# A 1-core transformer block: the first two modulation parts summed on TensorE in four column tiles, x loaded first, the first weights in narrower pieces

## The chip, the cores and the metric

The kernel runs on one core of a Trainium2 chip. The metric is device time in microseconds (us) of one execution, as the median of several. A profile of one execution gives the times of single instructions. Engines: TensorE (PE; its weight loads are PEld), VectorE (DVE), ScalarE (ACT), GpSimd (POOL) and SyncE (SP), which issues nearly all DMA transfers. Every engine works off its own list of instructions in order, so an instruction that waits holds up all that stand behind it on that engine.

## The reference, cut to what matters

Two layers of a block with D = 1024 and 256 tokens, all in float32. Each layer starts with six modulation rows made from a condition vector `c`; the first two (shift and scale) are needed before the first product of the mixer.

```python
cond = jax.nn.silu(c)                                  # [1, 1024]
mod = cond @ w_mod[l] + b_mod[l]                       # [1, 6*1024]; w_mod[l] is 1024 x 6144
sh1, sc1, g1, sh2, sc2, g2 = jnp.split(mod, 6, axis=-1)
h = _modulate(_rmsnorm(x, norm1_w[l]), sh1, sc1)       # norm * (1 + sc1) + sh1
y = _mixer(h, w_in[l], ...)                            # projections of h, three recurrent/attention branches
x = x + g1[:, None, :] * y
...                                                    # then a dense FFN (layer 0) or an 8-expert MoE (layer 1)
```

## The kernel before

Weights stream from HBM through a pool of four buffers `rawa` of 8 KB a partition (1 MB each), in the order in which units of work consume them. `Stream.loads` (L90) issues a load on SP as soon as a buffer is released; the order in which the instructions of different kinds follow one another on an engine is set by a scheduler when the program is built. The modulation weights of later parts go through two smaller buffers `rawm` (0.5 MB each).

A product with float32 weights is split in two: ACT copies a piece of weights to a rounded `wh` (L112), DVE subtracts to get the rest `wl` (L113), and TensorE sums three products (L517 to L519 with the activations first, L530 to L532 with them second). There are four pairs of `wh`/`wl`, and a unit of 256 output columns takes two of them, so the pairs of the next unit are made while TensorE works on this one. A unit has 48 matmuls. The first units are two of `b_f` (evacuated to `bf`), two of `b_q` (`bq`), two of `b_i` (`bi`), two of `b_g` (`bg`).

The start of the program, before the first product:

- `setup_cond` loads `c`, transposes it and forms `csil` = silu(c) (L278, L279). `setup_loads` (L283 to L288) brings norm weights and biases through six small transfers on POOL's queue; `setup_cols` transposes them (L292, L293) and ACT copies them to `pcol` and `bcol` (L294, L295).
- Parts 0 and 1 of layer 0: eight slices of 128 rows of `w_mod` each, two slices to a transfer of 1 MB (the last two of part 1 come singly). DVE adds each slice, times its entry of `csil`, into `macc` (L391, L393), eight operations of 128x1024 a part. `mod_done` then transposes `macc` in eight pieces on TensorE (L429), sums over the partitions on DVE (L430) and adds the bias (L431); after part 1 it forms `acol` (L435).
- Between them stands the norm of x: four squares with sums on ACT (`nsq`, L452), one sum on DVE (`nst`, L457), one power on POOL (`rr`, L273), two scaled identities on ACT (`dg`, L461), and 16 float32 products on TensorE that transpose and scale x (L473; the trace has two rows for each).
- `norm_T` applies `acol` and `modc` (`hf`, L486 on DVE and L488 on ACT) and splits the result in `hh` (ACT, L499) and `hl` (DVE, L500). The first product is L517.

A little later the first recurrent branch starts (`hgrn`, L592 to L600): ACT forms `he` in three steps (absolute value, exp, ln), DVE forms `hls` and `hkf` from it, ACT takes exp of `hkf`, and TensorE multiplies it (L630). Each change of function table on ACT is an instruction of its own, ACT_TABLE_LOAD. `setup_late`, which runs between the units, has some small exp and ln of its own (`lsm`, `lbe`).

The rest of the program (the mixer of layer 0, its FFN, the mixer of layer 1 and the experts) is in the same order before and after the change.

Of the kernel before, what the change touches and what calls it, by code (L numbers as in the profile page):

```python
# [15 lines left out]
OP = mybir.AluOpType  # L16
# [174 lines left out]
def _body(ctx, tc, nc, I, out):  # L191
# [76 lines left out]
    def rsqrt(pool, ss, n, scale, name):  # L268
# [5 lines left out]
        return r  # L274

    def setup_cond():
        p = ps_x()
        PE.transpose(out=p[:, 0:8], in_=prow2[0:8, :], identity=ident[0:8, 0:8])  # L278
        A.activation(out=csil, in_=p[:, 0:8], func=AF.Silu)  # L279

    def setup_loads():
# [93 lines left out]
    def mod_subs(l, part, ring, per, early=False):  # L375
# [3 lines left out]

        def step(k):  # L380
            def fn(src):
                if k == 0:
                    if l == 0 and part < 2:
                        st["acc"] = pools["s"].tile([128, D], F32, name="macc", tag="s")
                    else:
                        st["acc"] = pools["mac"].tile([128, D], F32, name="macc", tag="macc")
                    if part in (2, 5):
                        G.memset(st["acc"], 0.0)
                        SP.dma_start(out=st["acc"][0:1, :], in_=I["b_mod"][l:l + 1, part * D:(part + 1) * D])
# [5 lines left out]
                if k == 7:  # L395
                    if l == 0 and part < 2:
                        done(st["acc"])
                    else:
                        late.append([MD, lambda: done(st["acc"])])
            return fn  # L400
# [77 lines left out]
    def norm_T(pool, ps, l, which, dst):  # L478

        for j, pv in enumerate(ps):  # L480
# [8 lines left out]
            dst(j, hf)  # L489

    cur = {}

# [544 lines left out]
    def layer_mixer(l):  # L1037
# [7 lines left out]

        def t_unit(key, name, evac):
            raw = wchunk(W, COL[key], 512)

# [23 lines left out]
        def act(func):  # L1072
            return lambda o, i: A.activation(out=o, in_=i, func=func)
# [10 lines left out]

        seq = []
        r, f = t_unit("bf", "b_f", act(AF.Copy))
        cols_units(r, f, pre=lambda: norm_h(pools, l, 0))
        r, f = t_unit("bq", "b_q", act(AF.Silu))
# [569 lines left out]

    stream.unit([], first_norm, mods=list(mod_subs(0, 0, "a", 2)), alone=True)
    stream.unit([], lambda hi, lo: None, mods=list(mod_subs(0, 1, "a", 2, True)), alone=True)  # L1660
    n_mix = 2
# [16 lines left out]
    with tc.manual_schedule():  # L1678
        setup_cond()
        stream.loads()  # L1680
        SP.dma_start(out=x, in_=I["x"].rearrange("o (b p) d -> p (o b) d", p=128))
        setup_loads()
        setup_cols()
        stream.run(2, tick)
# [56 lines left out]
```

## Time and profile before

| | us |
|---|---|
| three runs | 1644.56, 1646.06, 1650.3 (median 1646.06) |
| the profiled execution | 1643.47 |
| its span, first to last instruction | 1641.8 |
| TensorE busy in the span | 1535.2 (94%) |
| VectorE, ScalarE, GpSimd busy | 764.9, 575.7, 42.5 |
| first weight product (L517) starts | 36.37 |

The span and the busy times are of the one profiled execution, which is 2.6 us faster than the median of the three runs; 1.67 us of it lie outside the span.

### The profile page before, as it was taken

The page shows a single profiled execution, that of the slowest core. Times are in us where ns is not written, and L with a number is a line of the kernel's source. Part 1 is how long each engine was busy: PE and PEld are TensorE (multiplying, and loading weights), DVE is VectorE, ACT ScalarE, POOL GpSimd, SP SyncE. Part 2 cuts the span into 40 slices and gives each one's busy share as a digit, 9 for nine tenths or more (in the row PEclk, how much of TensorE's full clock was granted, in tenths as well). Part 3 has the DMA queues.
Part 4 walks back from the last instruction along what each step waited for, and adds up shares of the span by engine and source line. Part 5 has one row for each costly group of instructions (what it writes and reads, how often), then busy time and mean ns, then how long its engine had stood idle before and what let it go on. Part 6 is the DMA issues. An engine that isn't in the chain of part 4 may idle for free. (4 is left out here: it accounts for less than half of the span.)

```text
span 1641.8 us, 25655 instructions
## 1 busy us (share of the span) xinstructions
PE 1535.2 (94%) x10586; PEld 1069.2 (65%) x10586; DVE 764.9 (47%) x1226; ACT 575.7 (35%) x904; POOL 42.5 (3%) x54
## 2 busy tenths in 40 slices
PE   3999999989999899999997999999999988987997
PEld 2999899989998899999996333433334322322332
DVE  7898788755877559865764010211012111111201
ACT  3576557645444487765752010100001000100000
POOL 2001020000000000001000000000000000000000
PEclk9999999999999999999998999999999999999999
DMA  9656777436789633654467799999899999999990
GB/s 361 231 177 217 244 267 259 155 103 226 240 296 320 228 129 129 219 168 154 155 214 299 260 352 354 407 406 321 319 329 407 403 408 405 407 403 407 404 372 36
DMA packets 162776, 459.25 MB, mean 280 GB/s; under 512 B 11454, under 2 KB 19716, under 8 KB 162600
## 3 DMA queue, kind: packets, MB, share of 16 engines
q1 hardware_dynamic: 162408, 456.55, 75.7%
q8 instruction: 140, 2.29, 0.6%
q14 instruction: 36, 0.29, 0.1%
q0 software_dynamic: 192, 0.11, 0.0%
HBM read 455.58 MB, written 1.05 MB: 278 GB/s over the span
## 5 line engine op out<-in xcount | busy, mean ns | idle before, releaser
L1463 PE MATMUL pm<-rawa,xg 128*64 128x512 f32 (+2 forms) x2368 | 417.8, 522 | 21.1 <-DMA rawa<-in_moe_w 18.6
L113 DVE TENSOR_TENSOR wl<-rawa,wh 128x1024 fp32r<-128x1024 f32 (+1 forms) x243 | 293.9, 1215 | 103.1 <-ACT wh L112 102.2
L112 ACT ACTIVATE wh<-rawa 128x1024 fp32r<-128x1024 f32 (+1 forms) x243 | 255.2, 1054 | 229.9 <-PE pm L518 117.3
L1463 PEld LDWEIGHTS pm<-rawa,xg 128*64 128x64 f32 (+1 forms) x2368 | 141.6, 131 | 280.0 <-issue 225.9
L517 PE MATMUL pm<-hh,wh 128*128 128x256 f32 x992 | 285.4, 288 | 4.8 <-ACT hh L499 4.6
L518 PE MATMUL pm<-hl,wh 128*128 128x256 f32 x992 | 283.8, 287 | 0.9 <-DVE hl L500 0.9
L519 PE MATMUL pm<-hh,wl 128*128 128x256 f32 x992 | 283.0, 286 | 1.5 <-DVE wl L113 1.5
L517 PEld LDWEIGHTS pm<-hh,wh 128*128 128x128 f32 x992 | 189.0, 191 | 8.1 <-ACT hh L499 4.8
L519 PEld LDWEIGHTS pm<-hh,wl 128*128 128x128 f32 x992 | 189.1, 191 | 2.4 <-DVE wl L113 1.9
L518 PEld LDWEIGHTS pm<-hl,wh 128*128 128x128 f32 x992 | 189.3, 191 | 1.9 <-DVE hl L500 1.4
L1463 PE MATMUL px<-rawa,gt 128*64 128x512 f32 x704 | 168.0, 600 | 12.5 <-DMA rawa<-in_moe_w 12.3
L1534 DVE TENSOR_TENSOR esg<-esg,pm 128x512 f32<-128x512 f32 (+1 forms) x48 | 29.5, 641 | 297.7 <-PE pm L1463 297.4
L531 PE MATMUL pm<-wl,hh 128*128 128x256 f32 x448 | 128.7, 287 | 1.6 <-DVE wl L113 1.6
L530 PE MATMUL pm<-wh,hh 128*128 128x256 f32 x448 | 128.8, 288 | 0.0
L532 PE MATMUL pm<-wh,hl 128*128 128x256 f32 x448 | 127.8, 285 | 0.0
L1463 PEld LDWEIGHTS px<-rawa,gt 128*64 128x64 f32 x704 | 46.1, 136 | 107.8 <-issue 83.8
L393 DVE SCALAR_TENSOR_TENSOR macc<-rawm,csil,macc 128x1024 f32<-128x1024 f32 x74 | 94.6, 1279 | 30.8 <-DMA rawm<-in_w_mod 30.1
L531 PEld LDWEIGHTS pm<-wl,hh 128*128 128x128 f32 x448 | 85.1, 190 | 2.0 <-DVE wl L113 1.8
L1561 DVE COPY ys<-pm 128x512 f32<-128x512 f32 x8 | 5.5, 691 | 173.2 <-PE pm L1463 93.9
L532 PEld LDWEIGHTS pm<-wh,hl 128*128 128x128 f32 x448 | 85.0, 190 | 0.2 <-issue 0.2
L530 PEld LDWEIGHTS pm<-wh,hh 128*128 128x128 f32 x448 | 85.0, 190 | 0.0
L1497 ACT ACTIVATE gt<-px 128x512 f32<-128x512 f32 (+1 forms) x24 | 13.5, 564 | 197.3 <-PE px L1495 197.3
(370 smaller groups left out, 1940.6 us busy)
## 6 DMA issues: line engine op xcount, KB each, us to landing
rawa<-in_moe_w SPq DMA_DIRECT2D x216, 1024.0 KB, 17.1
rawa<-in_w_in SPq DMA_DIRECT2D x68, 1024.0 KB, 6.3
rawa<-in_moe_w SPq DMA_DIRECT2D x64, 768.0 KB, 12.0
rawm<-in_w_mod SPq DMA_DIRECT2D x80, 512.0 KB, 7.6
rawa<-in_ffn_w SPq DMA_DIRECT2D x29, 1024.0 KB, 7.6
rawa<-in_w_branch SPq DMA_DIRECT2D x12, 1024.0 KB, 5.7
rawa<-in_w_out SPq DMA_DIRECT2D x8, 1024.0 KB, 5.7
rawa<-in_w_mod SPq DMA_DIRECT2D x7, 1024.0 KB, 10.2
```

What stands on the lines that cost most here:

```text
L112: nc.scalar.activation(out=hv, in_=src, func=AF.Copy)
L113: nc.vector.tensor_sub(out=lv, in0=src, in1=hv.bitcast(F32))
L393: V.scalar_tensor_tensor(out=st["acc"], in0=src[:, 0], scalar=csil[:, k:k + 1], in1=st["acc"], op0=OP.mult, op1=OP.add)
L517: PE.matmul(out=o, lhsT=wh, rhs=xh[:, k], start=(k == 0), stop=False)
L518: PE.matmul(out=o, lhsT=wh, rhs=xl[:, k], start=False, stop=False)
L519: PE.matmul(out=o, lhsT=wl, rhs=xh[:, k], start=False, stop=(k == nk - 1))
L530: PE.matmul(out=o, lhsT=xh[:, k, c], rhs=wh, start=(k == 0), stop=False)
L531: PE.matmul(out=o, lhsT=xh[:, k, c], rhs=wl, start=False, stop=False)
L532: PE.matmul(out=o, lhsT=xl[:, k, c], rhs=wh, start=False, stop=(k == nk - 1))
L1463: PE.matmul(out=bank[m * q:m * q + m, 0:c], lhsT=lhs(kind, k), rhs=w[:, k, c * q:c * q + c], start=first and k == 0, stop=last and k == 1)
L1497: A.activation(out=gT[g][:, i], in_=pv, func=AF.Copy)
L1534: V.tensor_tensor(out=gt[g][:, b, c], in0=gt[g][:, b, c], in1=hp[1][b][:, c], op=OP.mult)
```

## The change

Parts 0 and 1 of layer 0 are no longer summed by DVE. `setup_cond` now also spreads `csil` to a tile `cs` with every entry repeated 32 times. For each slice k TensorE runs four products (L390 of the new file) with `cs[:, k]` (128x32) as the stationary operand and 256 columns of the slice as the moving one; the four write to four groups of 32 partitions of one bank. After the eighth slice ACT copies the bank to `mrow` (L395), two transposes (L398) bring it to columns, and one DVE addition (L399) picks the columns and adds the bias; `acol` follows (L403).

The load of x stands ahead of the weight loads. The four 1 MB pieces of `w_in` for `b_f` become, in layer 0, four pieces of 0.5 MB of 256 columns each, two for each unit. The two parts now stand in one unit behind the norm of x.

```diff
@@ setup_cond
         A.activation(out=csil, in_=p[:, 0:8], func=AF.Silu)
+        cur["cs"] = pools["s"].tile([128, 8, 32], F32, name="cs", tag="t", bufs=TB)
+        V.tensor_copy(out=cur["cs"], in_=csil.unsqueeze(2).to_broadcast([128, 8, 32]))
@@ mod_subs
+        def first(k):
+
+            def fn(src):
                 if k == 0:
-                    if l == 0 and part < 2:
-                        st["acc"] = pools["s"].tile([128, D], F32, name="macc", tag="s")
-                    else:
-                        st["acc"] = pools["mac"].tile([128, D], F32, name="macc", tag="macc")
+                    st["p"] = ps_m()
+                for q in range(4):
+                    PE.matmul(out=st["p"][32 * q:32 * q + 32, 0:256], lhsT=cur["cs"][:, k],
+                              rhs=src[:, 0, 256 * q:256 * q + 256], start=(k == 0), stop=(k == 7))
+                if k < 7:
+                    return
+                t = pools["s"].tile([128, 256], F32, name="mrow", tag="t", bufs=TB)
+                A.activation(out=t, in_=st["p"][:, 0:256], func=AF.Copy)
+                p = ps_m()
+                for b in range(2):
+                    PE.transpose(out=p[:, 128 * b:128 * b + 128], in_=t[:, 128 * b:128 * b + 128], identity=ident)
+                V.tensor_tensor(out=modc[:, l, part].rearrange("p (q b) -> p q b", b=2),
+                                in0=p[:, 0:256].rearrange("p (b q i) -> p q b i", b=2, q=4)[:, :, :, 0],
+                                in1=bcol[:, 8 * part:8 * part + 8].rearrange("p (q b) -> p q b", b=2), op=OP.add)
...
+        def step(k):
+            if l == 0 and part < 2:
+                return first(k)
...
@@ layer_mixer
-        def t_unit(key, name, evac):
-            raw = wchunk(W, COL[key], 512)
+        def t_unit(key, name, evac, narrow=False):
+            if narrow:
+                raw = [wchunk(W, COL[key] + 256 * u, 256) for u in range(2)]
+            else:
+                raw = wchunk(W, COL[key], 512)
...
-        r, f = t_unit("bf", "b_f", act(AF.Copy))
-        cols_units(r, f, pre=lambda: norm_h(pools, l, 0))
+        r, f = t_unit("bf", "b_f", act(AF.Copy), l == 0)
...
@@ end of _body
-    stream.unit([], first_norm, mods=list(mod_subs(0, 0, "a", 2)), alone=True)
-    stream.unit([], lambda hi, lo: None, mods=list(mod_subs(0, 1, "a", 2, True)), alone=True)
+    stream.unit([], first_norm, alone=True)
+    stream.unit([], lambda hi, lo: None, mods=[*mod_subs(0, 0, "a", 2), *mod_subs(0, 1, "a", 2, True)], alone=True)
...
         setup_cond()
+        SP.dma_start(out=x, in_=I["x"].rearrange("o (b p) d -> p (o b) d", p=128))
         stream.loads()
-        SP.dma_start(out=x, in_=I["x"].rearrange("o (b p) d -> p (o b) d", p=128))
         setup_loads()
```

What stands in a row on an engine is shown at three places. In brackets are the engines or transfers that a row waits for; DMAHW0 to DMAHW7 are eight counters that SP's transfers use in turn, the one after the eighth the first again, and DMASW are POOL's transfers. A transfer that takes up a counter again waits until the last one on that counter has landed. The line numbers of the new file are higher by 4 to 30.

**SP, the first transfers.** Before, the fifth load of `w_mod` followed the load of x directly and waited for DVE to release the first buffer:

```order
L222 DMA prow_77<-in_c 8x128
L90 DMA rawa<-in_w_mod 128x2x1024 x4
L1681 DMA x_76<-in_x 128x2x1024
L90 DMA rawa<-in_w_mod 128x2x1024 [waits DMAHW1_49,DVE_49]
L90 DMA rawa<-in_w_mod 128x2x1024 [waits DMAHW2_49,DVE_49]
L90 DMA rawa<-in_w_mod 128x2x1024 [waits DMAHW3_49,DMAHW0_49,DVE_49]
L90 DMA rawa<-in_w_mod 128x1024 [waits DMAHW4_49,DVE_49]
L90 DMA rawa<-in_w_mod 128x1024 [waits DMAHW6_49,DVE_49]
L90 DMA rawa<-in_w_in 128x4x512 [waits DMAHW7_49,DVE_49]
```

Now the two `rawm` loads and seven small transfers stand between the fourth and the fifth load of `w_mod`:

```order
L222 DMA prow_77<-in_c 8x128
L1710 DMA x_76<-in_x 128x2x1024
L90 DMA rawa<-in_w_mod 128x2x1024 x4
L90 DMA rawm<-in_w_mod 128x1024 x2
L416 DMA macc<-in_b_mod 1x1024 [waits DMAHW0_49,Pool_49]
L302 DMA gb_81<-in_c_igate_b 4x2x1 [waits DMAHW1_49]
L303 DMA gb_81<-in_c_fgate_b 4x2x1 [waits DMAHW2_49]
L304 DMA rb_82<-in_moe_router_b 128x8 [waits DMAHW3_49]
L305 DMA rw_83<-in_moe_router_w 128x8x8 [waits DMAHW4_49]
L307 DMA prow_77<-in_a_knorm_w 2x2x64 [waits DMAHW5_49]
L307 DMA prow_77<-in_a_qnorm_w 2x2x64 [waits DMAHW6_49]
L90 DMA rawa<-in_w_mod 128x2x1024 [waits DMAHW7_49,PE_49]
```

The fifth load of `w_mod` now waits for DMAHW7, which is the second `rawm` load, and for TensorE instead of DVE.

**TensorE, from the setup to the first sums.** Before (names: `macc` the sums of DVE, `dg` the scaled identities of the norm):

```order
L292 MATMUL pm<-ident_84,prow_78 128x120 [waits DMASW4_49,DMASW3_49,DMASW5_49,DMASW2_49,DMASW1_49]
L293 MATMUL pm<-ident_84,brow_79 128x96 [waits DMASW0_49]
L429 MATMUL pm<-ident_84,macc 128x128 [waits DVE_49]
L429 MATMUL pm<-ident_84,macc 128x128 x7
L473 MATMUL px<-dg,x_76 128x128 [waits DMAHW5_49,Activation_49]
L473 MATMUL px<-dg,x_76 128x128 [waits Activation_49]
L473 MATMUL px<-dg,x_76 128x128 x14
L429 MATMUL pm<-ident_84,macc 128x128 [waits DVE_49]
L429 MATMUL pm<-ident_84,macc 128x128 x7
```

Now:

```order
L296 MATMUL pm<-ident_84,prow_78 128x120 [waits DMASW4_49,DMASW3_49,DMASW5_49,DMASW2_49,DMASW1_49]
L297 MATMUL pm<-ident_84,brow_79 128x96 [waits DMASW0_49]
L497 MATMUL px<-dg,x_76 128x128 [waits DMAHW1_49,Activation_49]
L497 MATMUL px<-dg,x_76 128x128 [waits Activation_49]
L497 MATMUL px<-dg,x_76 128x128 x14
L390 MATMUL pm<-rawa,cs 32x256 [waits DMAHW2_49,DVE_49]
L390 MATMUL pm<-rawa,cs 32x256 x7
L390 MATMUL pm<-rawa,cs 32x256 [waits DMAHW3_49]
L390 MATMUL pm<-rawa,cs 32x256 x7
L390 MATMUL pm<-rawa,cs 32x256 [waits DMAHW4_49]
L390 MATMUL pm<-rawa,cs 32x256 x7
```

The products of the norm (L473 before, L497 now) stand ahead of all sums of `w_mod`, which are now on this engine; the eight transposes of `macc` are gone.

**ACT, where the branch `hgrn` starts.** From the evacuation of the first `bq` unit on, ACT's list read before (`wh` are the weight pieces of the coming units):

```order
L1073 ACTIVATE bq<-pm 128x512
L1073 ACTIVATE bq<-pm 128x512 [waits PE_49]
L592 ACTIVATE he<-bf 128x1024 [waits Activation_49]
L320 ACT_TABLE_LOAD
L320 ACTIVATE lsm<-lsm 128x4 [waits DVE_49]
L333 ACTIVATE lbe<-lbe 128x8 [waits DVE_49]
L593 ACTIVATE he<-he 128x1024 [waits Activation_49]
L112 ACTIVATE wh<-rawa 128x1024 [waits DMAHW4_49,PE_49]
L348 ACT_TABLE_LOAD
L348 ACTIVATE lbe<-lbe 128x4 [waits DVE_49]
L594 ACTIVATE he<-he 128x1024 [waits Activation_49]
L112 ACTIVATE wh<-rawa 128x1024 [waits DMAHW5_49,PE_49]
```

and now:

```order
L1098 ACTIVATE bq<-pm 128x512 [waits PE_49]
L614 ACTIVATE he<-bf 128x1024 [waits Activation_49]
L324 ACT_TABLE_LOAD
L324 ACTIVATE lsm<-lsm 128x4 [waits DVE_49]
L337 ACTIVATE lbe<-lbe 128x8 [waits DVE_49]
L112 ACTIVATE wh<-rawa 128x1024 [waits PE_49]
L1098 ACT_TABLE_LOAD
L1098 ACTIVATE bq<-pm 128x512 [waits PE_49]
L352 ACT_TABLE_LOAD
L352 ACTIVATE lbe<-lbe 128x4 [waits DVE_49]
L615 ACT_TABLE_LOAD
L615 ACTIVATE he<-he 128x1024 [waits Activation_49]
```

The evacuation of the second `bq` unit (with a table load of its own) has moved in between the small exp and ln of `setup_late`, and the second step of `he` (L593, now L615) has moved behind the first `lbe` ln. Before these rows and up to the exp of `hkf` there were three table loads (L320, L348, L600); now there are six: the four seen here, one for the second `lbe` ln in the next row, and the one for `hkf`. On DVE, a `macc` addition of a `rawm` slice now stands between the second small `lbc` addition, which waits for that second ln, and the `wl` of the second half of the second `b_i` unit.

At the head of ACT's list nothing moved: `pcol`, `bcol` (L294, L295), then the four squares of x (L452), the two `dg` (L461), and now the two `mrow` copies behind them.

## Rows read from the trace of the kernel before

**Rows 1.** The page's first section: busy time of each engine in the span.
```profile
PE 1535.2 (94%) x10586; PEld 1069.2 (65%) x10586; DVE 764.9 (47%) x1226; ACT 575.7 (35%) x904; POOL 42.5 (3%) x54
```

**Rows 2.** Windows: length; busy PE, PEld, DVE, ACT, POOL (instructions); PE clock; DMA share; GB/s.
```profile
0.00:18.90 18.90, 2.25 (x10) 1.88 (x11) 11.15 (x11) 3.54 (x9) 6.32 (x21) 1.00 0.89 339
10.00:26.00 16.00, 6.12 (x26) 5.41 (x27) 14.16 (x16) 3.67 (x12) 1.08 (x1) 1.00 1.03 409
33.00:43.00 10.00, 5.78 (x25) 5.49 (x26) 9.90 (x22) 7.37 (x12) 0.55 (x2) 0.50 0.84 307
41.38:46.00 4.62, 4.62 (x33) 4.62 (x33) 3.19 (x12) 1.06 (x1) 0.00 (x0) 0.79 0.69 226
43.00:53.00 10.00, 10.00 (x84) 10.00 (x83) 8.37 (x16) 4.89 (x6) 0.00 (x0) 0.99 0.62 216
```

**Rows 3.** Timeline of the start (start, duration, engine, line, what): sums and first product.
```profile
8.86 14.21 SPq L90 DMA_DIRECT2D rawa<-in_w_mod  x5
...
21.41 9.21 DVE L393 SCALAR_TENSOR_TENSOR macc<-rawa,csil,macc 128x1024 f32<-128x1024 f32 x7
...
30.68 1.10 PE L429 MATMUL pm<-ident,macc 128*128 128x128 f32 x8 [2.61 <-DVE macc L393]
...
33.91 0.17 DVE L435 SCALAR_TENSOR_TENSOR acol<-modc,pcol 128x8 f32<-128x8 f32 x1
...
36.37 0.58 PE L517 MATMUL pm<-hh,wh 128*128 128x256 f32 x1 [4.59 <-ACT hh L499]
...
37.80 0.58 PE L518 MATMUL pm<-hl,wh 128*128 128x256 f32 x1 [0.85 <-DVE hl L500]
...
41.38 0.38 SPq L90 DMA_DIRECT2D rawa<-in_w_in  x1
```

**Rows 4.** Timeline of the start: the setup and the norm of x.
```profile
11.28 0.43 PE L292 MATMUL pm<-ident,prow 120*128 120x120 f32 x1 [8.58 <-DMA prow<-in_b_lb_logits]
...
12.07 0.24 ACT L295 ACTIVATE bcol<-pm 128x96 f32<-128x96 f32 x1
17.23 0.63 ACT L452 ACTIVATE nsq<-x 128x512 f32<-128x512 f32 x1 [4.91 <-DMA x<-in_x]
...
17.49 1.97 PE L429 MATMUL pm<-ident,macc 128*128 128x128 f32 x8 [5.62 <-DVE macc L393]
...
19.60 0.19 ACT L452 ACTIVATION_READ_ACCUMULATOR nsq<-x 128x1 f32 x1
...
20.37 0.15 DVE L457 TENSOR_REDUCE nst<-nss 128x2 f32<-128x4 f32 x1
...
20.88 1.08 POOL L273 TENSOR_TENSOR rr<-rv,mhalf 128x2 f32<-128x2 f32 x1 [13.92 <-DVE rv L272]
...
21.99 0.69 ACT L461 ACTIVATE dg<-ident,rr 128x128 f32<-128x128 f32 x2 [2.21 <-POOL rr L273]
...
22.45 5.62 PE L473 MATMUL px<-dg,x 128*128 128x128 f32 x32 [2.99 <-ACT dg L461]
```

**Rows 5.** Groups by line and form: mean ns; column tiles of the experts, and `wl`.
```profile
L113 DVE TENSOR_TENSOR wl<-rawa,wh 128x1024 fp32r<-128x1024 f32 x241 | 292.5, 1220 | 101.9 <-ACT wh L112 101.0
...
L1463 PE MATMUL pm<-rawa,xg 128*32 128x256 f32 x512 | 34.3, 385 | 0.0
```

**Rows 6.** Timeline of ACT where the branch `hgrn` starts, and one evacuation later.
```profile
57.54 1.06 ACT L112 ACTIVATE wh<-rawa 128x1024 fp32r<-128x1024 f32 x1 [0.38 <-PE pm L518]
...
66.64 1.28 ACT L320 ACT_TABLE_LOAD   x1
67.93 0.21 ACT L320 ACTIVATE lsm<-lsm 128x4 f32<-128x4 f32 x1
...
76.51 1.06 ACT L600 ACTIVATE hkf<-hkf 128x1024 f32<-128x1024 f32 x1
...
135.90 0.64 ACT L1129 ACTIVATE cv<-pm 128x256 f32<-128x256 f32 x2
```

**Rows 7.** Waits in the first 80 us (engine, line, releaser: total, times, longest).
```profile
PE px L630 <- ACT hkf L600: 1.8, 1, 1.8
```

More of the change, by code (lines that the diff above doesn't have):

```diff
@@ L274, in rsqrt @@
         return r
+    cur = {}
     def setup_cond():
@@ L378, in mod_subs @@
         done = mod_done(l, part)
-        def step(k):
+        def first(k):
             def fn(src):
                 if k == 0:
-                    if l == 0 and part < 2:
-                        st["acc"] = pools["s"].tile([128, D], F32, name="macc", tag="s")
-                    else:
-                        st["acc"] = pools["mac"].tile([128, D], F32, name="macc", tag="macc")
+                    st["p"] = ps_m()
[12 more added lines that the diff above has]
+                                in1=bcol[:, 8 * part:8 * part + 8].rearrange("p (q b) -> p q b", b=2), op=OP.add)
+                if part == 1:
+                    V.scalar_tensor_tensor(out=acol[:, l, 0], in0=modc[:, l, 1], scalar=1.0,
+                                           in1=pcol[:, N1W:N1W + 8], op0=OP.add, op1=OP.mult)
+            return fn
+        def step(k):
+            if l == 0 and part < 2:
+                return first(k)
+            def fn(src):
+                if k == 0:
+                    st["acc"] = pools["mac"].tile([128, D], F32, name="macc", tag="macc")
                     if part in (2, 5):
@@ L395, in fn @@
                 if k == 7:
[L396 to L399, printed above, removed]
+                    late.append([MD, lambda: done(st["acc"])])
             return fn
@@ L489, in norm_T @@
             dst(j, hf)
-    cur = {}
     def norm_h(pools, l, which):
@@ L1085, in layer_mixer @@
         seq = []
-        r, f = t_unit("bf", "b_f", act(AF.Copy))
-        cols_units(r, f, pre=lambda: norm_h(pools, l, 0))
+        r, f = t_unit("bf", "b_f", act(AF.Copy), l == 0)
+        if l == 0:
+            for u in range(2):
+                cols_units(r[u], (lambda _, hi, lo, u=u: f0(u, hi, lo)), pre=(lambda: norm_h(pools, l, 0)) if u == 0 else None)
+            f0 = f
+        else:
+            cols_units(r, f, pre=lambda: norm_h(pools, l, 0))
         r, f = t_unit("bq", "b_q", act(AF.Silu))
```

## The prediction, made before the changed kernel was run

> **What bounds the kernel now.** I read the busy times first: TensorE is busy for 94% of the span and no other engine for half of it [rows 1]. So I looked for places where TensorE stands idle, since only these can pay, and whether a gain there would last. The timeline of the start shows the largest one: the first weight product begins at 36.37 us, the second at 37.80, and from there TensorE works nearly without a break. What ends last ahead of it is a chain on DVE: it adds the slices of part 1 in one piece from 21.41 to 30.62, TensorE transposes, `acol` is done at 34.08, the activations follow [rows 3]. DMA runs at its full rate of 409 GB/s in that time [rows 2], and the loads of `w_mod` go out as early as 8.86 [rows 3]: nothing there waits for a buffer for long, and DVE is the slower of the two. A second idle piece is small: the first product of the branch `hgrn` waits 1.8 us for ACT's exp of `hkf` [rows 7].
>
> Behind the start, the lists of all engines agree with those of before apart from a few places within the first mixer, and whatever follows is paced by TensorE or starts its loads when TensorE has freed something. So a shift at the start reaches the end one to one. The sum is therefore a shift of the first unit's end, plus what happens where `hgrn` starts.
>
> **The change part by part.**
>
> *The sums.* DVE loses sixteen additions; one takes 1.32 us (9.21 for seven) [rows 3]. TensorE gets 64 products in four tiles of 32 columns. The experts' stage has the same form (128x32 stationary, 128x256 moving, float32): 34.3 us busy for 512, so 0.067 us each, with 0.385 for one alone [rows 5]. Eight of them, for one transfer of 1 MB, take 0.385 + 7 x 0.067 = 0.85 us at the full clock and about 1.7 at half. The transfer takes 1.049 MB / 409 = 2.56 us [rows 2]. The sums are no longer the bound at either clock; the transfers are.
>
> *x first.* The norm cannot start when x arrives: on ACT its squares stand behind `pcol` and `bcol`, which wait for the transposes of POOL's small loads at 11.28, and `bcol` ends at 12.31 [rows 4]. From there I take the steps of before: the squares 17.23 to 19.79, 2.56 us; from the DVE sum to POOL's power 20.88 - 20.37 = 0.51; from there to `dg` 21.99 - 20.88 = 1.11; to the first product 22.45 - 21.99 = 0.46; the products 5.62 [rows 4]. That gives 12.31 + 2.56 + 0.51 + 1.11 + 0.46 = 16.95 for the start of the norm's products and 22.6 for their end. Before, they ran from 22.45 to 28.07 beside DVE's sums and delayed nothing.
>
> *What is queued behind them.* On TensorE all sums now stand behind these products. The first two slices can be summed from 22.6 to 23.5, though they landed by about 9, and only then is the first `rawa` buffer free. On SP, the fifth load of `w_mod` waits for that buffer (and for the second `rawm` load on its counter). So SP issues it at 23.5 and not at 8.86 [rows 3], and all that stands behind it, the rest of `w_mod` and the first `w_in`, with it.
>
> *The transfers.* By then SP has issued x, four pieces of `w_mod` and two of `rawm`: 6 x 1.049 = 6.29 MB, with POOL's loads some 6.4 MB. The first 18.9 us of before moved 339 x 18.9 = 6.4 MB [rows 2]. So DMA runs dry at 18.9 and stands for 4.6 us, plus the time that a transfer needs to get under way on an empty queue. For that the trace has one piece: a load of 1 MB issued at 41.38 [rows 3] had moved its 226 x 4.62 = 1.04 MB by 46.0 [rows 2], so at most 4.62 - 2.56 = 2.06 us beyond its streaming; I take 1.9 (bounds 1.0 and 2.06). The remaining 4.19 MB of `w_mod` take 10.25 us, so the last slice lands at 23.5 + 1.9 + 10.25 = 35.7.
>
> *From the last slice to `acol`.* At half clock four products take 2 x (0.385 + 3 x 0.067) = 1.17; the copy `mrow` 0.32, half of the two 128x256 copies in 0.64 [rows 6], 0.1 for the hand-overs; two transposes 2 x 0.25 (eight took 1.97) [rows 4]; the addition and `acol` 0.17 each [rows 3] with hand-overs 0.45. Sum 2.6: `acol` at 38.3 instead of 34.08, **+4.2**. At full clock the products take 0.59 and the transposes 0.28 (eight in 1.10) [rows 3]: 1.75, and +3.4. I take half clock: in the stretch of short, broken work from 33 to 43 the granted clock was 0.50 [rows 2], and the sums are short pieces between landings. From `acol` on, the steps are those of before, except that `wh` and `wl` of the unit's second half are now made behind `hh` and `hl`, since their narrower pieces land later: **+0.2** by counting the products out by the time that this `wl` is ready (16 now, 17 before).
>
> *Narrower pieces.* Four loads of 0.5 MB land 1.3 us after one another from the last slice on, sooner than ACT and DVE can split them (1.06 and 1.22 us a piece [rows 5, 6], and the activations stand between): 0. Should short rows stream at half the rate, the first `wh` would hold up the activations by about 1 us.
>
> *Where `hgrn` starts.* Counted from the start of the second `wh` for `b_i` (57.54 before), the exp of `hkf` ended at 77.57, 20.0 us later [rows 6]. Now ACT has three more table loads of 1.28 each [rows 6] in that stretch. In its new order: `wh` 1.06, `bq` 0.5, `he` 1.0, load, two small ones; then a `wh` that must wait for TensorE and ends at 5.4; load, `bq`, load, `lbe`, load, `he`, load, `lbe` to 12.5; `wh` to 13.55. DVE has a `macc` addition (1.32) between the last `lbc` and the `wl` of that piece, which ends at 12.5 + 0.2 + 1.3 + 1.22 = 15.3. TensorE, at 0.119 a product (84 in 10.00) [rows 2], wants it at 13.1 and so stands for 2.2 us. It then ends that unit at 19.5; ACT's next `wh` waits for it until 18.1 and ends at 19.15, load to 20.4, exp of `hkf` to 21.5. Against 20.0 that is **+1.5**; bounds 0 (if the loads were covered) and 3.85 + 1.32 = 5.2 (all on the path). The Trainium skill, "ScalarE: Activation LUTs", section "What ACT_TABLE_LOAD costs", gives about 1.38 us of drain on top of each load, which would make these three loads cost 4.1 us more; but the row shows the next ACTIVATE 0.01 us behind the load's end (66.64 + 1.28, then 67.93) [rows 6], so the trace disagrees.
>
> *Small ones.* `cs` is one copy of 128x256 at 3 us, in DVE's idle time. Two `macc` additions of the `rawm` slices run while DVE waits: 0 at the start, and DVE has that much less to do later, where it is not what TensorE waits for.
>
> **Sum.** 4.2 + 0.2 + 1.5 = 5.9 us on the profiled 1643.47 (its span of 1641.8 and 1.67 around it): 1649.4. The median of the three runs, 1646.06, is 2.6 above the profiled execution; the same shift gives 1652. The kernel gets slower by 0.36%. About 0.3%, 4.9 us, is what a measurement of this kernel can tell from no change.
>
> **The rivals.**
>
> *The clock stays high* through the sums and into the first unit. `acol` is then at +3.4, and the first unit gains up to 0.9, as its first 16 products are held up by `wl` anyway. Sum 3.4 - 0.9 + 1.5 = 4.0: 1650, no change. For it: the norm's products run right ahead of the sums. Against it: pauses of some 2 us between landings. The Trainium skill, "TensorE: Matmul & The Clock Gate", section "HAM oscillation — how this bites in real kernels", says that a kernel whose bursts are parted by DMA waits starts each of them slow; no run here shows it for these sums.
>
> *ACT's loads are covered* where `hgrn` starts: 5.9 - 1.5 = 4.4: 1650.5, no change. For it: DVE has less to do there. Against it: the count above.
>
> *DMA does not run dry* (not slower): if the norm started when x lands, near 6 us, the sums would free the first buffer before the second `rawm` load lands at 18.9, and the fifth load would go out at 19.0. That takes 4.5 off: +1.4, 1647.5, no change. It decides from a release before 22.5 on, where the sum falls under 4.9. Against it: ACT's order, `bcol` at 12.31.
>
> *All table loads are on the path*: 5.2 in place of 1.5, so +9.6, 1655.7, slower.
>
> **How the numbers follow.** Forecast 0.50 (its own range 1650 to 1655), clock high 0.17, loads covered 0.14, DMA not dry 0.10, all loads on the path 0.06; 0.03 remain for a gain of over 0.3%, which none of these gives even together (4.0 - 1.5 - 4.5 = -2.0). The forecast lies only 1 us above the bound, so 0.12 of its 0.50 goes to no change; a third of the next two goes to slower. Slower 0.38 + 0.10 + 0.06 = 0.54 and, with rounding, 0.55; same 0.41; faster 0.04. The range 1647 to 1657 takes in the third and the fourth rival.
>
> **What would show it.** Right: the first `w_mod` sum at about 22.6, right behind the norm's products; SP's fifth `w_mod` load at about 23.5; no DMA traffic from about 19 to 25; `acol` near 38, the first weight product near 40.7; three more table loads around 65 to 80 and an idle TensorE of about 3.5 us there. Wrong: a first sum before 19, DMA without a gap, or a first product before 36.

## The result, and the profile after the change

The changed kernel takes 1655.2 us (median of 7 runs, 1651.74 to 1657.32), the kernel before 1644.94 in the same comparison (7 runs, 1640.93 to 1650.3). The ratio is 1.0059, with a 95% interval of 1.0042 to 1.0077: slower by 0.6%, some 9.7 us by the ratio (the two medians lie 10.3 apart). Forecast were 1652 (1647 to 1657) and +5.9 us. The profiled execution took 1653.17 us, its span is 1650.9.

The timeline of the changed kernel, the rows that answer to [rows 3, 4, 6] (start, duration, engine, line, what, in brackets the idle time before it and what ended it):

```profile
11.93 0.63 ACT L476 ACTIVATE nsq<-x 128x512 f32<-128x512 f32 x1
...
16.24 6.06 PE L497 MATMUL px<-dg,x 128*128 128x128 f32 x32 [4.64 <-ACT dg L485]
22.23 3.66 PE L390 MATMUL pm<-rawa,cs 128*32 128x256 f32 x64
23.36 7.99 SPq L90 DMA_DIRECT2D rawa<-in_w_mod  x5
...
29.87 1.07 PE L390 MATMUL pm<-rawa,cs 128*32 128x256 f32 x16 [2.98 <-DMA rawa<-in_w_mod]
...
32.42 1.93 PE L390 MATMUL pm<-rawa,cs 128*32 128x256 f32 x16 [1.48 <-DMA rawa<-in_w_mod]
...
34.99 3.39 PE L390 MATMUL pm<-rawa,cs 128*32 128x256 f32 x32 [0.64 <-DMA rawa<-in_w_mod]
...
37.53 0.22 PEld L390 LDWEIGHTS pm<-rawa,cs 128*32 128x32 f32 x8 [0.64 <-DMA rawa<-in_w_mod]
...
39.63 0.17 DVE L403 SCALAR_TENSOR_TENSOR acol<-modc,pcol 128x8 f32<-128x8 f32 x1
...
42.06 0.58 PE L539 MATMUL pm<-hh,wh 128*128 128x256 f32 x1 [2.67 <-ACT hh L521]
...
68.54 1.28 ACT L1098 ACT_TABLE_LOAD   x1
...
74.34 1.28 ACT L352 ACT_TABLE_LOAD   x1
75.64 0.21 ACT L352 ACTIVATE lbe<-lbe 128x4 f32<-128x4 f32 x1
75.75 1.04 ACT L112 ACTIVATE wh<-rawa 128x1024 fp32r<-128x1024 f32 x1
...
85.42 1.06 ACT L622 ACTIVATE hkf<-hkf 128x1024 f32<-128x1024 f32 x1
```

The sums begin right behind the norm's products and free the first buffer then; the fifth load of `w_mod` goes out at 23.36. Its products start 6.5 us later, the next loads follow at the full rate (2.55 apart), the last slice's weights enter TensorE at 37.53, and `acol` is done at 39.80, 5.72 later than before [rows 3]. In the windows of the changed kernel (columns as in [rows 2]) DMA has nothing to move from 20 to 24 us; the later ones are those around `hgrn` and one at 230 us:

```profile
18.00:19.00 1.00, 1.00 (x7) 1.00 (x7) 0.00 (x0) 0.00 (x0) 0.00 (x0) 1.00 1.04 371
19.00:20.00 1.00, 1.00 (x6) 1.00 (x6) 0.56 (x1) 0.00 (x0) 0.00 (x0) 1.00 0.57 33
20.00:24.00 4.00, 4.00 (x53) 3.19 (x55) 2.01 (x2) 0.00 (x0) 0.00 (x0) 1.00 0.00 0
24.00:25.00 1.00, 1.00 (x24) 0.63 (x20) 0.00 (x0) 0.00 (x0) 0.00 (x0) 1.00 0.84 94
25.00:26.00 1.00, 0.89 (x20) 0.26 (x8) 0.00 (x0) 0.00 (x0) 0.00 (x0) 1.00 0.68 197
26.00:28.00 2.00, 0.44 (x2) 0.20 (x2) 0.17 (x1) 0.38 (x1) 0.00 (x0) 1.00 1.00 397
28.00:35.00 7.00, 3.01 (x34) 1.02 (x34) 0.00 (x0) 0.00 (x0) 0.00 (x0) 0.73 1.02 415
...
36.00:38.00 2.00, 2.00 (x28) 0.65 (x20) 0.00 (x0) 0.00 (x0) 0.00 (x0) 0.50 0.74 252
...
76.00:78.00 2.00, 0.48 (x2) 0.19 (x1) 2.00 (x4) 2.00 (x3) 0.00 (x0) 1.00 0.00 0
78.00:80.00 2.00, 1.50 (x8) 1.50 (x9) 2.00 (x3) 2.00 (x3) 0.00 (x0) 0.74 0.27 27
80.00:82.00 2.00, 2.00 (x12) 2.00 (x11) 2.00 (x3) 0.11 (x1) 0.00 (x0) 0.50 0.90 316
82.00:84.00 2.00, 2.00 (x17) 2.00 (x17) 2.00 (x4) 0.95 (x1) 0.00 (x0) 0.91 1.06 421
...
230.00:235.00 5.00, 5.00 (x35) 5.00 (x34) 3.35 (x4) 1.09 (x2) 0.00 (x0) 0.75 0.00 0
```

What TensorE waits for in two stretches, 44 to 92 us (the first three rows) and 160 to 315 us (the last): groups by line of the changed kernel, with count, busy time and mean ns, then the idle time ahead of them and its releaser.

```profile
L552 PE MATMUL pm<-wh,hh 128*128 128x256 f32 x45 | 13.6, 301 | 0.8 <-ACT wh L112 0.8
L553 PE MATMUL pm<-wl,hh 128*128 128x256 f32 x44 | 13.2, 301 | 1.3 <-DVE wl L113 1.3
...
L652 PE MATMUL px<-bq,hkf 128*128 128x128 f32 x16 | 2.1, 281 | 1.4 <-ACT hkf L622 1.4
...
L591 PE MATMUL px<-ident,myt 128*128 128x128 f32 x8 | 3.2, 420 | 3.4 <-DVE myt L878 3.4
```

At `hgrn` TensorE now waits 3.5 us in three places; before, it waited 1.8 in one [rows 7]. And from 78 to 84 us it runs at half clock for part of the time (0.50 is 1.2 GHz), right behind two of these waits (0.75 us for `wh`, then 1.27 for `wl`, which ends at 78.50). Before, the granted clock was 1.00 in every window from 74 to 88 us, in the one with the wait of 1.8 us too:

```profile
76.00:78.00 2.00, 0.38 (x3) 0.39 (x4) 2.00 (x3) 1.99 (x4) 0.00 (x0) 1.00 0.28 106
```

To see how the loss builds up, I compare the end of the same ACT instruction in two traces: the second evacuation of `bf` (53.33 us before, the second unit's end), the first `ci` (159.34, behind `hgrn`), and the fourth `aaT` (299.45, late in the first mixer). The table gives these ends against the trace of before, with the end of `acol` and the span; e1 to e11 are the runs of the next section. The last column is the timed ratio to the kernel before, with its 95% interval.

| kernel | `acol` | `bf` | `ci` | `aaT` | span | ratio |
|---|---|---|---|---|---|---|
| changed | 39.80 | +5.35 | +8.0 | +11.75 | +9.1 | 1.0059 (1.0042 to 1.0077) |
| e8, changed again | 40.14 | +5.9 | +8.6 | +10.3 | +9.7 | one run |
| e1 part 0's sums first | 36.14 | +4.5 | +4.4 | +7.0 | +4.4 | 1.0024 (1.0007 to 1.0042) |
| e2 `pcol`, `bcol` late | 35.12 | +0.8 | +1.15 | +3.4 | +1.6 | 0.9994 (0.9979 to 1.0009) |
| e3 wide pieces | 39.72 | +8.6 | +7.6 | +7.3 | +2.7 | 1.0044 (1.0028 to 1.0061) |
| e4 before, x first | 36.79 | +1.7 | +7.8 | +8.0 | +8.7 | 1.0059 (1.0042 to 1.0076) |
| e5 `setup_late` moved | 40.35 | +6.2 | +4.9 | +16.0 | +19.0 | 1.0071 (1.0057 to 1.0084) |
| e6 e4 and that move | 36.65 | +2.4 | +3.7 | +10.5 | +7.3 | 1.0065 (1.0051 to 1.0079) |
| e7 three loads ahead | 31.90 | -3.1 | -1.3 | +2.6 | +1.7 | 0.9991 (0.9982 to 1.0000) |
| e9 half pieces | 41.65 | +6.6 | +7.8 | +11.6 | +10.0 | 1.0072 (1.0052 to 1.0092) |
| e10 e7, whole pieces | 31.42 | -2.1 | -2.2 | +1.4 | -0.3 | 0.9984 (0.9972 to 0.9996) |
| e11 e10, wide | 31.48 | -1.8 | -1.9 | -1.1 | -4.4 | 0.9984 (0.9973 to 0.9995) |

Two things have to be kept in mind with this table. The ends and spans are those of one execution each, and some of these lie far from their median: that of e3 is the fastest of its twelve (by 4.9 us against the median), that of e5 the slowest of its six (by 7.5). And the runs differ in two places at once: up to the exp of `hkf` ACT loads six tables in the changed kernel, e4, e8 and e9, five in e3, and three, as before the change, in e1, e2, e5, e6, e7, e10 and e11. So `acol` and `bf` tell what an edit did to the start; the times also hold what the order at `hgrn` costs.

So the changed kernel loses 5.35 us at the start and 2.65 more up to `ci`. Behind that point the lists of TensorE and ACT agree with those of before, and the difference still moves by some microseconds; e8 takes that up.

### The profile page after: what moved, and what is told of

It is laid out like the page before. It is cut to its first block, busy times and chain, and to the rows that moved or that the text cites. A ratio compares the mean times of both kernels' runs of the same rounds, so it can differ in the third digit from the quotient of the medians.

```text
span 1650.9 us, 25866 instructions
## 1 busy us (share of the span) xinstructions
PE 1546.7 (94%) x10702; PEld 1075.7 (65%) x10702; DVE 743.8 (45%) x1207; ACT 580.5 (35%) x909; POOL 42.2 (3%) x54
## 3 DMA queue, kind: packets, MB, share of 16 engines
HBM read 455.58 MB, written 1.05 MB: 277 GB/s over the span
## 5 line engine op out<-in xcount | busy, mean ns | idle before, releaser
L1493 PE MATMUL px<-rawa,gt 128*64 128x512 f32 x704 | 167.5, 600 | 10.3 <-DMA rawa<-in_moe_w 10.2
```

Source lines behind the costliest of these rows:

```text
L1493: PE.matmul(out=bank[m * q:m * q + m, 0:c], lhsT=lhs(kind, k), rhs=w[:, k, c * q:c * q + c], start=first and k == 0, stop=last and k == 1)
```

## The experiments

Four questions: is the start late because DMA runs dry (theory A) or because of the sums themselves (B); do the narrow pieces cost anything (D); do the table loads cost the time at `hgrn` (E, with rival F); and why did DMA's restart cost more than forecast (H, I)? Two further rivals, C and G, are stated with the runs that they belong to.

**e1: the sums of part 0 ahead of the norm's products.**

```diff
-    stream.unit([], first_norm, alone=True)
-    stream.unit([], lambda hi, lo: None, mods=[*mod_subs(0, 0, "a", 2), *mod_subs(0, 1, "a", 2, True)], alone=True)
+    stream.unit([], first_norm, mods=list(mod_subs(0, 0, "a", 2)), alone=True)
+    stream.unit([], lambda hi, lo: None, mods=list(mod_subs(0, 1, "a", 2, True)), alone=True)
```

> The changed kernel with the sums of part 0 put ahead of the norm's products on TensorE. Theory A (the start is late because the sums stand behind the norm's products, so the first buffer is freed late and DMA runs dry): the sums begin behind the transposes of POOL's loads at about 11.6 us, SP's fifth w_mod load goes out near 13 (changed kernel: 23.36), DMA has no gap at 20 to 24. The norm now waits for mrow on ACT and its products run near 23 to 29; behind them the last slice's load goes out near 30 and lands near 33.4, so acol comes at about 35.5 (changed kernel 39.8, before 34.08). Table loads are as in before, so the shift against before at 167 us is 1 to 2 us and the time is about 1647. Rival B (the sums themselves, as short pieces at half clock with their hand-overs, are what is slow): acol stays beyond 38.5 and the time within 2 us of the changed kernel's 1655.

The sums began at 11.75, the fifth load of `w_mod` went out at 13.74, the norm's products ran from 22.93 to 29.45, the ninth load went out at 30.51, and `acol` came at 36.14, within 0.7 us of theory A's figure. Rival B is out. At the second unit's end 4.5 us were lost all the same, more than `acol`'s 2.1, and at `ci` 4.4 where 1 to 2 had been forecast; the time, 1648.0, is 1 us above the forecast. Two rows of e1, the last products of the sums and what ACT did next:

```profile
34.00 0.64 PE L390 MATMUL pm<-rawa,cs 128*32 128x256 f32 x8 [1.39 <-DMA rawa<-in_w_mod]
...
37.30 1.06 ACT L112 ACTIVATE wh<-rawa 128x1024 fp32r<-128x1024 f32 x1 [2.15 <-DMA rawa<-in_w_in]
```

The first `w_in` load stands behind that ninth load and went out at 31.38. ACT stood 2.15 us for its `wh`, and the norm's activations stand behind that on ACT, so that the first weight product started at 39.84, 3.5 us later than before.

**e2: the norm no longer behind `pcol` and `bcol`.**

```diff
+        stream.run(1, tick)
         setup_cols()
-        stream.run(2, tick)
+        stream.run(1, tick)
```

> The changed kernel with the transposes and copies of POOL's small loads (pcol, bcol) put behind the norm; sums still behind the norm's products. Theory A: the squares start when x lands, near 6.5 us, the norm's products run near 11.2 to 17.2, the sums begin near 18, SP's fifth w_mod load goes out near 18.8, so DMA hardly runs dry, the last slice lands near 30.1 and acol comes at 32.4 to 34. Shift against before at the first unit's end -1.5 to +0.5 us, time 1644 to 1648. Rival B (sums on TensorE are the slow part): acol beyond 37. Rival C (x does not land before about 10 us, as four more loads share the queues with it): no more than 2 us are won.

The timeline of e2:

```profile
10.64 6.61 PE L497 MATMUL px<-dg,x 128*128 128x128 f32 x32 [8.01 <-ACT dg L485]
...
17.37 3.66 PE L390 MATMUL pm<-rawa,cs 128*32 128x256 f32 x64
...
18.50 8.78 SPq L90 DMA_DIRECT2D rawa<-in_w_mod  x5
...
24.95 1.93 PE L390 MATMUL pm<-rawa,cs 128*32 128x256 f32 x16 [2.92 <-DMA rawa<-in_w_mod]
```

Everything up to the fifth load is as theory A said, and the kernel is level with the one before (0.9994). `acol` is 1.1 us later than the forecast's upper end: the load at 18.50, for which DMA stood hardly a microsecond, again needs 6.45 us until its products start. Rivals B and C are out.

**e3: the first weights in pieces of 512 columns again.**

```diff
-        r, f = t_unit("bf", "b_f", act(AF.Copy), l == 0)
+        r, f = t_unit("bf", "b_f", act(AF.Copy))
+        cols_units(r, f, pre=lambda: norm_h(pools, l, 0))
```

> The changed kernel with the first weights in pieces of 512 columns again. Theory D (rows of 1 KB slow the queue while the last slices come in): the last products of the sums start 1 to 1.8 us earlier than in the changed kernel (37.53), the DMA rate stays near 400 GB/s from 35 to 39 us, acol at 38 to 38.8. Against that, the first two weights land later, so the unit's end may win less. Rival: the restart of the empty queues alone is slow, acol unchanged at 39.8. One table load less in the stretch of hgrn than in the changed kernel (5 for 6 up to hkf's exp). Time 1652 to 1655.

The last slice's weights entered TensorE 7.69 us behind those of the fifth load (29.54 to 37.23), in the changed kernel 7.66 (29.87 to 37.53): theory D falls, the narrow pieces cost nothing there. Without them the second unit's end is 3.2 us later: the first product waits for its `wh` and starts at 45.39 instead of 42.06. At `ci` the two kernels are 0.4 apart, and their timed ratios can't be told apart.

**e4: the kernel before, with x loaded first and nothing else.**

```diff
+        SP.dma_start(out=x, in_=I["x"].rearrange("o (b p) d -> p (o b) d", p=128))
         stream.loads()
-        SP.dma_start(out=x, in_=I["x"].rearrange("o (b p) d -> p (o b) d", p=128))
```

> The kernel before with x loaded first and nothing else; the sums stay on DVE. DVE is the bound at the start, its first slice lands 2.56 us later, of which at most 0.7 falls into a wait, and the norm's two small DVE steps move out of its way: acol at 35.5 to 36.5 (before 34.08). The list of ACT gets the same order of table loads around hgrn as in the changed kernel (six up to hkf's exp, not three). Theory E (these loads cost the time where hgrn starts): from the first unit's end to hkf's exp 2 to 3.3 us longer than before, shift at 167 us of 4 to 5, time 1649. Rival F (they are hidden, the changed kernel loses there for another reason): no more than 0.5 us longer, shift at 167 us of 2, time 1647.

This one line makes the kernel as slow as the whole change does (1.0059). `acol` came at 36.79, 2.7 us late and 0.3 above the forecast, and the second unit ended 1.7 late. From there to `ci` it lost 6.1 us, about twice what theory E gave; rival F (hidden loads) is out. Groups by line of e4, 44 to 92 us, and its windows:

```profile
L530 PE MATMUL pm<-wh,hh 128*128 128x256 f32 x46 | 14.1, 307 | 3.8 <-ACT wh L112 3.8
L531 PE MATMUL pm<-wl,hh 128*128 128x256 f32 x46 | 14.0, 305 | 0.7 <-DVE wl L113 0.7
...
L630 PE MATMUL px<-bq,hkf 128*128 128x128 f32 x16 | 2.1, 281 | 1.4 <-ACT hkf L600 1.4
```

```profile
74.00:76.00 2.00, 0.00 (x0) 0.00 (x0) 0.33 (x2) 1.99 (x3) 0.00 (x0) 0.76 0.00 1
76.00:78.00 2.00, 1.05 (x3) 0.76 (x4) 1.75 (x2) 2.00 (x3) 0.00 (x0) 0.50 0.00 0
78.00:80.00 2.00, 2.00 (x11) 2.00 (x11) 2.00 (x3) 1.54 (x3) 0.00 (x0) 0.50 0.67 194
80.00:82.00 2.00, 2.00 (x12) 2.00 (x11) 2.00 (x4) 0.00 (x0) 0.00 (x0) 0.54 1.07 394
```

TensorE waits 5.9 us instead of 1.8, which makes 4.1; in the changed kernel one `wh` stands between the loads, here it stands behind five of them. The clock comes on top: it goes to 1.2 GHz while TensorE waits, and the work done at 0.50 and 0.54 from 76 to 82 loses 1.05 x 0.5 + 2 x 0.5 + 2 x 0.46 = 2.4 us by this estimate. Together that is 6.5 us, where 6.1 were lost. Theory E named the place; its price of 2 to 3.3 us was short of the waits alone and lacked the clock.

**e5, e6: the same list of loads as before the change.** `setup_late` goes behind `setup_masks` and one step later, in the changed kernel (e5) and in e4 (e6):

```diff
-        setup_late(pools["s"])
-        yield
         setup_masks(pools["s"])
         yield
+        yield
+        setup_late(pools["s"])
+        yield
```

> The changed kernel with the small setup steps (setup_late) issued behind setup_masks and one step later; the start up to the first unit is the same. ACT then loads three tables up to hkf's exp, as before the change, and not six. Theory E (the three added loads and the order of ACT around them cost the time where hgrn starts): the shift against before stays at 5.5 to 6.2 us from the first unit's end to 167 us (changed kernel 8.0), no wait of TensorE for wh or wl there, time about 1652. Rival F (they are hidden, and the 2.4 us come from the weights' splits that start late): shift at 167 us still 8, time 1655.

> The kernel before with x loaded first, as in the fourth run, and with setup_late issued behind setup_masks and one step later: three table loads up to hkf's exp in place of six. Theory E: the shift at the first unit's end stays 2.7 us as in the fourth run, and it is still no more than 3.5 at 167 us (fourth run 7.8); the waits of 3.8 us on wh and 0.7 on wl are gone; time 1646 to 1647. Rival F: shift at 167 us still 7 to 8, time 1653.

Up to `ci` theory E holds. In e5 the waits around `hgrn` are 1.1 us (`wh`) and 0.7 (`hkf`), as much as before the change; the clock stays full, and from `bf` to `ci` it gains 1.3 us where the changed kernel loses 2.65. In e6 the waits are 2.8 us, the clock falls behind them (0.75, 0.50 and 0.90 from 86 to 92 us), and the loss falls from 6.1 to 1.25. The times missed: 1655.1 and 1653.2, no better than without the edit. Both lose 7 to 11 us between `ci` and `aaT`, where the moved setup changed other orders (how much of e5's 11 belongs to that one execution, the slowest of its six, a single profile can't tell); groups by line of e5, 160 to 315 us:

```profile
L962 PE MATMUL px<-ident,at 128*128 128x128 f32 x12 | 3.2, 319 | 4.0 <-DVE at L950 4.0
L591 PE MATMUL px<-ident,myt 128*128 128x128 f32 x8 | 2.9, 420 | 5.2 <-DVE myt L878 5.2
```

The wait for `myt` is 5.2 us (3.4 in the changed kernel), and one of 4.0 for `at` is new; in e6 they are 3.9 (2.4 in e4) and 3.3. So these two runs show what the loads cost at their place and no way to win it back.

**e7: three loads summed ahead of the norm's products, `pcol` and `bcol` behind them.** The edit is that of e2 and

```diff
-    stream.unit([], first_norm, alone=True)
-    stream.unit([], lambda hi, lo: None, mods=[*mod_subs(0, 0, "a", 2), *mod_subs(0, 1, "a", 2, True)], alone=True)
+    first = [*mod_subs(0, 0, "a", 2), *mod_subs(0, 1, "a", 2, True)]
+    stream.unit([], first_norm, mods=first[:6], alone=True)
+    stream.unit([], lambda hi, lo: None, mods=first[6:], alone=True)
```

> The changed kernel with the sums of the first three loads ahead of the norm's products, and pcol and bcol behind them. By theory A the first buffers come free at about 10, 12.5 and 15, the norm's products run near 15 to 22, SP's ninth w_mod load goes out near 23.5, DMA has no gap, the last slice is summed from about 27.5 and acol comes at 30 to 31 (before 34.08, changed kernel 39.8): shift against before -3 to -4 us at the first unit's end and at 167 us, time 1639 to 1640, ratio 0.9975. Rival B (the sums on TensorE at half clock and their hand-overs bound the start, not the loads): acol not before 33.5, time 1643 or more. Rival G (w_in's narrow pieces come too late for the earlier acol): acol at 30 but the first unit's end no earlier than 1 us before that of before.

`acol` came at 31.90, 7.9 us earlier than in the changed kernel, and the second unit ended 3.1 us earlier than before the change: A against B is settled, and rival G falls. The last load waits for the buffer of the fifth one; its weights entered TensorE 2.36 us behind the load ahead of it. The lead does not last. At `hgrn` TensorE waits 1.9 us for `hkf`, hardly more than before, but here the clock falls behind that wait:

```profile
76.00:78.00 2.00, 2.00 (x15) 2.00 (x14) 2.00 (x4) 1.15 (x2) 0.00 (x0) 0.66 0.89 270
78.00:80.00 2.00, 2.00 (x11) 2.00 (x11) 2.00 (x4) 0.39 (x1) 0.00 (x0) 0.50 0.13 27
```

That is 2 x 0.34 + 2 x 0.5 = 1.7 us, about the 1.8 that are lost up to `ci`; more is lost by `aaT`, and of the 4 us forecast 1.5 are left in the time (0.9991, an interval that reaches 1).

**e8: the changed kernel once more**, for the difference that moves behind `ci`; no edit.

> The changed kernel once more, for a second profile. The shift against before grew from 8.0 us at 167 us to 12 at 300 and fell back to 9.1 at the end, with the lists of all engines alike there. If the granted clock falls at the same places and for as long as in the first profile, this growth belongs to the program (how its shifted work meets the clock); if its places and lengths differ, the 4 us between are scatter of one execution, and only the shift at 167 us is the change's own.

It differs. In the first profile 3.75 us came on between `ci` and `aaT`, in the second 1.7; from 230 to 235 us the first ran at a granted clock of 0.75 (above), the second at full clock:

```profile
230.00:235.00 5.00, 5.00 (x44) 5.00 (x44) 3.72 (x4) 2.06 (x3) 0.00 (x0) 1.00 0.00 2
```

So about 2 us there are scatter of one execution. Both runs lose between `ci` and `aaT`, though, and in both TensorE's wait for `myt` is longer than the 2.1 us of before (3.4 and 2.4); whether the rest belongs to the program two profiles can't tell.

**e9: all of part 1 in loads of 0.5 MB.**

```diff
-mods=[*mod_subs(0, 0, "a", 2), *mod_subs(0, 1, "a", 2, True)], alone=True)
+mods=[*mod_subs(0, 0, "a", 2), *mod_subs(0, 1, "a", 1)], alone=True)
```

> The changed kernel with all of part 1 in loads of 0.5 MB (eight, not three of 1 MB and two of 0.5). It tells apart why the restart of DMA cost 3.95 us beyond streaming (issue 23.36, first products 29.87, 2.56 of it streaming) and not the 1.9 of the forecast. Theory H (a lag that comes with the size of a load; in the first run a load of 0.5 MB on a queue that stood still took only 2.2 beyond streaming): the first products of part 1 start near 26.9, the last slice's near 35.8, acol near 38 and the shift at 167 us falls to 6 to 6.5. Theory I (the same lag for any load): the first products near 28.6, the last slice's still at 37.5, acol 39.8, shift 8 to 8.6.

The first products of part 1 started at 28.18, the last slice's at 38.91: theory I is nearer, H falls, and `acol` (41.65) is later than both said. The lag behind the issue beyond streaming is 28.18 - 23.48 - 1.28 = 3.4 us. The last slice is 1.4 us later than in the changed kernel; the four buffers now hold half as much in flight, but whether that is the reason was not tried. Ratio 1.0072.

e9 also tells something about `hgrn`. Behind the second unit its lists of TensorE, ACT and DVE are those of the changed kernel, and TensorE's three waits are the same (0.8, 1.3 and 1.4 us). But its clock stays full behind them:

```profile
78.00:80.00 2.00, 0.58 (x2) 0.39 (x3) 2.00 (x4) 2.00 (x4) 0.00 (x0) 1.00 0.00 0
80.00:82.00 2.00, 2.00 (x18) 2.00 (x18) 2.00 (x3) 1.41 (x2) 0.00 (x0) 1.00 0.48 96
```

From `bf` to `ci` it loses 1.2 us. The changed kernel loses 2.65 and e8 2.7, both with the clock down to 0.50. So in these three executions some 1.5 us of the loss there come and go with the clock.

**e10, e11: e7 with part 1 in four whole loads (e10), and the wide first weights in addition (e11, with e3's edit).**

```diff
-    first = [*mod_subs(0, 0, "a", 2), *mod_subs(0, 1, "a", 2, True)]
+    first = [*mod_subs(0, 0, "a", 2), *mod_subs(0, 1, "a", 2)]
```

> The seventh run's kernel with part 1 loaded in four pieces of 1 MB, so that its last slices wait for the buffer of part 0's fourth load and not of the fifth load (in the seventh run that last load went out near 24.5 and its products started at 29.85, 2.36 behind the ones before). Theory A: the last products start near 28.0 to 28.5, acol at 30 to 31, first weight product 32.5 to 33.3, shift against before -3.5 to -4.5 us at the first unit's end (seventh run -3.1); at 167 us it depends on the stall where hgrn starts and on the clock behind it: -2 to -4, time 1640 to 1642. Rival: part 1 as a whole is bound by DMA's rate from the start on, the last products no earlier than 29.5, shift -3 as in the seventh run.

> The tenth run's kernel with the first weights in pieces of 512 columns. If the narrow pieces help the earlier start, the first weight product comes 0.5 to 1 us later than in the tenth run, and its unit's end too; if they only change ACT's order, the first product is within 0.3 us and the unit's end as well. Time 1640 to 1643.

The timeline of e10:

```profile
9.49 1.94 PE L390 MATMUL pm<-rawa,cs 128*32 128x256 f32 x16 [6.84 <-DMA rawa<-in_w_mod]
...
16.61 5.93 PE L497 MATMUL px<-dg,x 128*128 128x128 f32 x32
...
28.94 1.07 PE L390 MATMUL pm<-rawa,cs 128*32 128x256 f32 x16 [1.47 <-DMA rawa<-in_w_mod]
...
34.26 0.58 PE L539 MATMUL pm<-hh,wh 128*128 128x256 f32 x1 [3.25 <-ACT hh L521]
```

Here the norm's products run while DMA brings the next loads (397 to 418 GB/s from 18 to 23 us, where the changed kernel has none from 20 to 24). The last products started at 28.94, 0.4 us later than forecast, `acol` came at 31.42, the first weight product at 34.26 and not by 33.3, and the second unit ended 2.1 us earlier than before the change, not 3.5 to 4.5. At `hgrn` the wait is 1.5 us, the clock stays full, and the lead is kept up to `ci` (2.2). At 0.9984 with an interval just below 1 e10 is faster than the kernel before, by 0.16%, and e11 likewise; that is less than the 0.3% that the prediction took for what a measurement can tell. The first products of e10 and e11 (34.26, 34.23) agree, and the second units' ends lie 0.33 us apart: with an early `acol`, too, the narrow pieces do not show in the time.

## Why the prediction was right, and which of its terms were off

*The start, right in its mechanism.* The norm behind `bcol`, the sums behind the norm, the first buffer at 23.5 (23.36), the dry DMA from 19 to 24 and half clock under the last sums (0.50 from 36 to 38; part 0's ran at 1.00) came as forecast; e1, e2 and e7 move `acol` as this chain says. Mis-sized was one term, "plus the time that a transfer needs to get under way on an empty queue": 1.9 us forecast, 6.51 - 2.56 = 3.95 measured. The row from which it came told when the bytes had moved, not when a reader could start. The trace of before had the other figure too: it marks the end of that load of 41.38 with 16 signals, and the last of them came at 47.32, 47.32 - 41.38 - 2.56 = 3.4 us beyond streaming. In the changed kernel 94 + 197 + 2 x 397 = 1085 KB had moved from 24 to 28 us, as much as the fifth load has; its products started at 29.87, right behind the last of its 16 signals (29.82). So the last slice entered TensorE at 37.53 and not at 35.7. From it to `acol` 2.27 us passed, forecast 2.6 (its terms as listed add up to 2.54). The term behind `acol`, +0.2, had the wrong sign: `acol` is 5.72 late, the first unit's end 4.8 (4.4 forecast), and the second's, `bf`, 5.35.

*The narrow pieces*: 0 forecast, 0 at the last slice (e3), and they help the first two units; at `ci` and in the time nothing of that is left.

*Where `hgrn` starts.* The waits were sized right: 3.5 us instead of 1.8 is +1.7, forecast +1.5. Missing was what can follow on them: behind the first two the clock falls, and the work at 0.74, 0.50 and 0.91 (78 to 84 us) loses 1.5 x 0.26 + 2 x 0.5 + 2 x 0.09 = 1.6 us. Together 3.3; from `bf` to `ci` 2.65 were lost, so 0.65 were won back in places that I did not trace. In e9, where the same waits left the clock full, 1.2 were lost, near the forecast.

*The sum.* 5.35 + 2.65 = 8.0 at `ci`, against 5.9. The ratio says 9.7; what lies between came behind `ci`, and it is partly scatter (e8). The sum also took for granted that a shift at the start reaches the end one to one. It does not: e3 was 8.6 us late at `bf` and 7.6 at `ci`, and of e7's lead of 3.1 us about half was left in the time.

*What was luck.* The time, 1655.2, lies inside the stated range, but just above the 1650 to 1655 that the forecast had for itself. The range reached further up for the rival with all table loads on the path, and its +9.6 is almost the 9.7 measured, by chance: that rival puts 5.2 us at `hgrn`, where the trace has 2.65, and nothing behind it.

*The rivals.* The clock did not stay high; ACT's loads were not covered. "DMA does not run dry" is what e2 nearly builds: +1.4 was its price (-0.1 with the three table loads that e2 has), -1.0 was measured (-3.5 to +1.5 by the interval). "All table loads are on the path" is not what the changed kernel does; e4 comes nearer to it, with 4.1 us more of waits.

What the prediction did not see: the move of the x load alone reorders ACT's list at `hgrn`, and mostly by that costs as much as the whole change, with the sums left on DVE. The sums on TensorE need not be a loss: placed as in e10 they end level with the kernel before or 0.16% under it. How much of that is theirs is not shown, since no run has the sums on DVE with x first and the norm ahead of `pcol` and `bcol`.

## What to carry to other kernels

Work that releases load buffers should not be moved behind other work on the same engine: what it costs is the queue's standstill and then the lag of its restart, 2.2 to 3.95 us in the runs of this kernel. Take such a lag from a row that pairs the issue with its reader, not from the bytes. And when a load is moved, compare the lists of all engines far behind it: in e4 the larger price stood some 70 us behind the moved load, in the order of ACT's table loads, and undoing it there made new waits still further on.

## What the runs showed of the hardware that I had not expected

*The lag of a load on a queue that had run empty or nearly so.* From issue to the reader, beyond streaming, it was 3.95 us (changed), 3.89 (e2), 3.4 (e9) and, for the last load of 0.5 MB in e1, only 34.00 - 30.51 - 1.28 = 2.2. The Trainium skill, "DMA: Bandwidth & Descriptors", section "Anatomy of one DMA — SWDGE (gpsimd) path", gives about 2.0 us of fixed cost, most of it the receipt behind the last byte. It is written for another issuing engine; e1 agrees with its size, the other three runs don't. The traces show what most of the difference is. The end of every one of these loads is marked by 16 signals, and the reader started some 0.05 us behind the last. Fifteen signals had come 3.0 (changed), 2.4 (e2), 2.7 (e9) and 2.1 us (e1) beyond streaming; the sixteenth came 0.9, 1.5, 0.65 and 0.06 us later. In the changed kernel the last signal also came 0.9 us behind the others in each of the four loads that followed, so the last slice and `acol` were late by it. Why one signal is late, and not in e1, no run shows.

*The clock behind a wait.* In the changed kernel (both profiles), e4, e6 and e7 TensorE's clock fell to 1.2 GHz at or behind its waits at `hgrn`: 0.75 and 1.27 us in the changed kernel, 1.9 in e7, 3.8 in e4. Before the change a wait of 1.8 us at that place, and in e2 one of 2.3, left it at full clock, and so did e10's of 1.5:

```profile
74.00:76.00 2.00, 0.49 (x5) 0.28 (x4) 2.00 (x4) 1.99 (x3) 0.00 (x0) 1.00 1.08 366
76.00:78.00 2.00, 2.00 (x18) 2.00 (x19) 1.51 (x4) 1.81 (x2) 0.00 (x0) 1.00 0.21 23
```

In e9 the same waits as in the changed kernel left it at full clock as well. So the length of the wait alone does not decide it here; what does, these runs don't tell.
